# One weight piece split earlier, second norm's statistics as a product with ones, and last layer norm's transposes later, in a hybrid decoder layer

## The chip, the core and the metric

The kernel runs on one core of a Trainium2 chip. The core has five engines with queues of their own, each working through its instructions in order: TensorE (PE; the loading of its weights is shown as PEld), VectorE (DVE), ScalarE (ACT), GpSimd (POOL) and SyncE (SP, which here only starts transfers). PE writes into PSUM; DVE, ACT and POOL work on SBUF, and DVE and ACT also read PSUM. An instruction that needs another engine's result waits for a semaphore, and everything behind it on its engine waits too. The metric is the time of one execution in microseconds (us), the median of several runs.

## What is computed

One decoder layer on 512 tokens of width 2048, in float32. All activations are held transposed: 128 channels on the partitions, 512 tokens along a row.

```python
def reference(x, ...):
    h = rms_norm(x, mix_norm_g[l])
    p = h @ w_in[l]                               # 2048 x 5136
    a_val, a_gate, q, k, v, z, b_raw, a_raw = jnp.split(p, splits, axis=-1)
    out_a = conformer_conv_group(...)             # GLU, conv of 31 taps, layer norm per 128 channels, silu, product
    out_b = gated_deltanet_group(...)             # gated delta rule, chunks
    x = x + jnp.concatenate([out_a, out_b], axis=-1) @ w_out[l]
    h = rms_norm(x, ffn_norm_g[l])                # the second norm
    gate, up = jnp.split(h @ w_up[l], 2, axis=-1) # 2048 x 11264
    gate = causal_depthwise_conv(gate, ffn_conv_w[l]) + ffn_conv_b[l]
    x = x + (jax.nn.silu(gate) * up) @ w_down[l]
    return rms_norm(x, final_norm_g)

def rms_norm(x, g):
    return x * lax.rsqrt(jnp.mean(x * x, axis=-1, keepdims=True) + EPS) * g
```

## The kernel before

Every large product is done in three passes. A weight and an activation are each split into a rounded high half and the remainder: ACT casts the high half (`whi`, `uhi`), DVE subtracts it from the float32 value to get the low half (`wlo`, `ulo`). `mm3` then issues high x high, high x low and low x high, in this order: the first two of three matmuls need only the high half of the weight, the third needs the low one. A **weight piece** is 512 columns of one weight tile, thus four blocks of 128 x 128 and twelve matmuls. `split_piece()` issues the cast and the subtraction of the next piece; the pieces wait in `pieces` until a product takes them. There are four buffers for `hi` and four for `lo`.

The stages in order of time: the input projection with the delta rule and the convolutions beside it; `w_out` for the half that comes from the delta rule (`acc<-obh`), while the last convolution and its layer norm still run; the pointwise product `pw` (`acc<-yh`, 8 tiles); `w_out` for the convolution's half (`acc<-ah`), in the loop `for i, m in enumerate(PAIRS)`, which adds the result to the token tile `xv`; the up projection; the down projection.

The last tile of that loop gives the last token tile. Its consumers are the token operands of the up projection, made by `operand_a` and `operand_b`: ACT scales (`h`), casts (`xb`, `xt`), DVE forms differences (`d`) and low halves. The up projection (`up_out` and the loop `for f in range(NF)`, 44 rounds) computes two rows of two tiles with seven products in place of eight, which is why DVE also adds and subtracts raw weights (`wraw<-uraw,wraw` and the like). In round 0 the products come in the order 11 (into `bx`), 12 (`bv`), 22 (`bz`), s1 and s3 (both halves of `by`), s2 (`bx`), s4 (`bz`), each of 24 matmuls of 256 columns from two pieces; round 1 begins 11 (`bx`), 22 (`bz`), 12 (`bv`), s1 (`by`). Pieces 1 to 4 of round 0 come from `split_piece`, the later ones from `up_products`.

After the seventh product `up_out` multiplies the gate by `rstd2`, the 512 values 1/sqrt(mean square + eps) repeated on all 128 partitions: `fg<-g,rstd_bc` on DVE, once per round. `rstd2` comes from `rms_stats`: four products of the summed squares `sqsum` with a column of ones put the tokens on partitions (128 x 4), DVE scales (`ms`), POOL raises to the power -0.5 (`rstd<-ms,mhalf`), four products with the identity (`statb`) spread the result over the partitions, and ACT copies it to SBUF.

The order of instructions on each engine is fixed when the program is recorded. `Flow` keeps a model clock of each engine; tasks are generators in a heap, `fl.spawn(task, delay)` starts one at a model time, `yield N(tile)` lets it sleep until the model says that the tile is ready, and `fl.tick()` after each `mm3` lets due tasks issue. The model decides only the order; on the chip the semaphores decide the times. `fl.drain(op_ev)` lets the model run until the token operands are issued.

Of the kernel before, what the change touches and what calls it, by code (L numbers as in the profile page):

```python
# [18 lines left out]
ALU = mybir.AluOpType  # L19
AX = mybir.AxisListType  # L20

P = 128
T = 512
NB = 4
D = 2048
KT = D // P
CH = 1024
NC = CH // P
# [7 lines left out]
EPS = 1e-6  # L36
# [9 lines left out]
D_LEFT, D_RIGHT = 40, 4  # L46
SPLIT_TILES = 1
BA_LAG = 3
WARM = 12
ENGINES = {getattr(mybir.EngineType, n) for n in ("PE", "DVE", "Activation", "Pool", "SP")}  # L50

# [240 lines left out]
def N(*aps):  # L292
    return aps, False


def S(*aps):
    return aps, True
# [9 lines left out]
def tile_trunk(ctx: ExitStack, tc: tile.TileContext, xT, w_k, w_ba, w_m, pw, w_out, w_up, w_down, par_d, cst_d, out):  # L307
    nc = tc.nc
    fl = Flow(nc)
    V, ACT, POOL, SP = fl.vector, fl.scalar, fl.gpsimd, fl.sync  # L310
# [19 lines left out]
    def nm(s):  # L330
        uid[0] += 1
        return f"{s}_{uid[0]}"
# [22 lines left out]
    def misc(name="misc"):  # L355
        return fl.tile(misc_ps, [P, T], F32, "misc", 4, nm(name))
# [6 lines left out]
    def alloc(tag, name, shape):  # L363
        fl.live[tag] += 1
        if tag == "misc":
            t = misc(name)
        elif tag == "acc":
            t = fl.tile(acc_ps, [P, T], F32, "acc", 4, nm(name))
        elif tag == "DE":
            t = DE(name, shape)  # L370
        elif tag == "s3":
            t = B(tag, name, shape=(P, 256))
        else:
            t = B(tag, name)
        owner[t.tensor.name] = tag
        return t
# [6 lines left out]
    def turn(tag, n):  # L383
        q = queues.setdefault(tag, deque())
        me = object()
        q.append(me)
        while q[0] is not me or room(tag) < n:
            yield 0.2
        q.popleft()

    def G(tag, name, shape=None):
        yield from turn(tag, 1)
        return alloc(tag, name, shape)
# [5 lines left out]
    def free(*tiles):  # L399
        for t in tiles:  # L400
            fl.live[owner.pop(t.tensor.name)] -= 1
            fl.freed.add(t.tensor.name)
# [6 lines left out]
    def pc(n, i=0, w=1):  # L409
        return par[:, OFF[n] - KT + i : OFF[n] - KT + i + w]  # L410

    def cc(n, w):
        return cst[:, COFF[n] : COFF[n] + w]
# [4 lines left out]
    ones = cc("ones", P)  # L418
    m32 = cc("m32", 64)
    sel = cst[0:32, COFF["sel"] : COFF["sel"] + 16]  # L420
    mhalf = cpool.tile([P, 32], F32, name="mhalf")
# [5 lines left out]
    wps = misc("warm")  # L427
    for _ in range(WARM):
        fl.matmul(wps, lhsT=wz[:, 0:P], rhs=wz)
# [22 lines left out]
    def load_next():  # L452
        i = len(raws)
        if i < (len(plan) if up_done else up_at + 3):
            src, n, step = plan[i]
            raw = fl.tile(wpool, [P, 1024], F32, "raw", 3, nm("wraw"))
            for o in range(0, n, n if i else step):
                e = o + (n if i else step)
                SP.dma_start(raw[:, o:e], src[:, o:e])
            raws.append(raw)  # L460

    def split_piece():
        i, o = nsplit
        if i >= len(plan):
            return
        if i == up_at + 2:
            have = len(pieces)
            for _ in up:
                if len(pieces) > have:
                    return  # L470
                yield
            nsplit[:] = [i + 1, 0]
            i, o = nsplit
        n, step = plan[i][1:]
        w = min(step, n - o)
        src = raws[i][:, o : o + w]
        if i >= len(plan) - 3 * SPLIT_TILES:
            hi, lo = DT("whi"), DT("wlo")
        else:
            hi = fl.tile(wpool, [P, 512], F32R, "hi", 4, nm("whi"))  # L480
            lo = fl.tile(wpool, [P, 512], F32R, "lo", 4, nm("wlo"))
        ACT.copy(out=hi[:, :w], in_=src)
        yield
        V.tensor_tensor(out=lo[:, :w], in0=src, in1=hi[:, :w].bitcast(F32), op=ALU.subtract)
        pieces.append((hi, lo))
        if o + w < n:
            nsplit[1] = o + w
        else:
            nsplit[:] = [i + 1, 0]
            load_next()  # L490
# [97 lines left out]
    def rms_rows(parts, blocks, lag=0.0):  # L588
        yield N(*parts)
        ps = yield from G("misc", "stat")  # L590
        for b in blocks:
            for i, t in enumerate(parts):
                fl.matmul(
                    ps[:, b : b + 1], lhsT=t[:, blk(b)], rhs=ones[:, 0:1], start=i == 0, stop=i == len(parts) - 1)
        n, b0 = len(blocks), blocks[0]
        ms = sm("ms", NB, pool=cpool)
        V.tensor_scalar(out=ms[:, 0:n], in0=ps[:, b0 : b0 + n], scalar1=1.0 / D, scalar2=EPS, op0=ALU.mult, op1=ALU.add)
        free(ps)
        r = rsqrt_pow(ms[:, 0:n], n, "rstd", cpool)
        yield N(r)  # L600
        yield lag
        ps2 = yield from G("misc", "statb")
        for i in range(n):
            fl.matmul(ps2[:, blk(i)], lhsT=r[:, i : i + 1].to_broadcast([P, P]), rhs=ident)
        return r, ps2

    def rms_stats(total, bcast, lag=0.0):
        r, ps2 = yield from rms_rows([total], range(NB), lag)
        ACT.copy(out=bcast, in_=ps2)
        free(ps2)  # L610
        return r

    def rstd_tile(name):
        return fl.tile(cpool, [P, T], F32, "rstdb", 1, name)
# [14 lines left out]
    total = None  # L629
# [37 lines left out]
    for k in range(KT):  # L667
# [9 lines left out]
        if total is None:  # L677
            total = B("cf", "sqsum")
            ACT.activation(out=total, in_=xs, func=AF.Square)
        else:  # L680
            add_square(xs, total, xtmp)
        if k == BA_LAG:
            split_ba()
        if k >= BA_LAG:
            for j in range(0 if k == BA_LAG else k, k + 1):
                ba_product(j)
# [423 lines left out]
    ln_ev = [Event() for _ in range(NC)]  # L1110
# [18 lines left out]
    def conv31(c, u):  # L1129
        a = yield from G("ca", "cacc")  # L1130
        yield S(u)
        ACT.activation(
            out=a, in_=u, func=AF.Identity, scale=pc("dw_w", c * TAPS + TAPS - 1), bias=pc("dw_b", c))
        yield S(a)
        for s in range(1, TAPS):
            V.scalar_tensor_tensor(
                out=a[:, s:], in0=u[:, : T - s], scalar=pc("dw_w", c * TAPS + TAPS - 1 - s), in1=a[:, s:],
                op0=ALU.mult, op1=ALU.add)
            yield 1
        free(u)  # L1140
        fl.spawn(layer_norm(c, a), 0.0, ln_ev[c])

    def layer_norm(c, a):
        tp = yield from transpose4(a)
        free(a)
        bn = sm("bn", NB * 6, 1, pool=bpool)
        mv = sm("mv", NB * 2, pool=bpool)
        for b in range(NB):
            V.bn_stats(out=bn[:, b * 6 : (b + 1) * 6], in_=tp[:, blk(b)])
        for b in range(NB):  # L1150
            V.bn_aggr(out=mv[:, b * 2 : (b + 1) * 2], in_=bn[:, b * 6 : (b + 1) * 6])
        mv2 = mv.rearrange("p (b c) -> p b c", c=2)
        va = sm("va", NB, pool=bpool)
        V.tensor_scalar_add(va.unsqueeze(2), mv2[:, :, 1:2], EPS)
        rl = rsqrt_pow(va, NB, "rl", bpool)
        yield S(rl)
        nmr = sm("nmr", NB, pool=bpool)
        V.scalar_tensor_tensor(
            out=nmr.unsqueeze(2), in0=mv2[:, :, 0:1], scalar=-1.0, in1=rl.unsqueeze(2), op0=ALU.mult, op1=ALU.mult)
        n = yield from G("cf", "lnn")  # L1160
        yield S(nmr)
        for b in range(NB):
            ACT.activation(
                out=n[:, blk(b)], in_=tp[:, blk(b)], func=AF.Identity, scale=rl[:, b : b + 1], bias=nmr[:, b : b + 1])
        free(tp)
        tp2 = yield from transpose4(n)
        free(n)
        y = yield from G("y", "y")
        yield S(tp2)
        ACT.activation(out=y, in_=tp2, func=AF.Silu, scale=pc("ln_g", c), bias=pc("ln_b", c))  # L1170
        SP.dma_start(scr_y[c], y)
        free(tp2, y)
# [79 lines left out]
    for m in PAIRS:  # L1252
        t = fl.tile(opool, [P, T], F32, "xo", 4, nm("xo"))
        SP.dma_start(t, xT[m])
        ps = mtile(obhl)
# [5 lines left out]
    for m in range(NC):  # L1261
        ps = mtile(yhl)
# [3 lines left out]
            out=lo, in0=ps, scalar=pc("pw_b", m), in1=hi.bitcast(F32), op0=ALU.add, op1=ALU.subtract)  # L1266
# [14 lines left out]
    def DT(name):  # L1281
        for pool, n in dpools:
            if fl.live[id(pool)] < n:
                fl.live[id(pool)] += 1
                t = fl.tile(pool, [P, T], F32R, "d", n, nm(name))
                owner[t.tensor.name] = id(pool)
                return t
# [60 lines left out]
    total = [None]  # L1348
# [6 lines left out]
    for i, m in enumerate(PAIRS):  # L1355
        load_xv()
        ps = mtile(ahl)
# [4 lines left out]
        op_ev.append(fl.spawn((operand_b if i % 2 else operand_a)(i // 2, t)))  # L1362
        op_ev.append(fl.spawn(square(t), 1.5))
    rstd2 = rstd_tile("rstd2_bc")
    fl.drain(op_ev)
    fl.spawn(rms_stats(total[0], rstd2, 3.0), 6.0)
    tctx.close()
    actx.close()
    upool = uctx.enter_context(tc.tile_pool(name="up", bufs=1, side="right", reuse_waits="tile"))
# [178 lines left out]
    for f in range(NF):  # L1548
# [7 lines left out]
        for n, w in enumerate(products_of(f)):  # L1556
            b, c, x = products[w]
# [105 lines left out]
    total = None  # L1663
    for m in range(KT - SPLIT_TILES):
        down(1, m)
        total = add_square(x2[m], total, L)
# [110 lines left out]
```

## Time and profile before

| | |
|---|---|
| runs | 2162.17, 2164.89, 2166.77 us, median 2164.89 |
| profiled execution | 2164.05 us, of it 2162.2 us from the first to the last instruction |
| mean granted TensorE clock | 0.996 of full speed |
| busy in the span | PE 2142.8 us (99%), DVE 1626.1 (75%), ACT 956.6 (44%), POOL 60.6 (3%) |
| chain that ended last | PE 95%, DVE 2%, DMA 1% |

The profiled execution is one run, 0.8 us under the median. PE is busy nearly all the time, so what shortens or lengthens the kernel is what PE waits for, and what PE itself does. Matmul rows are pipelined: the distance from one start to the next, and not the row's duration, is what a matmul costs PE. All instructions are recorded in one helper, so their line is always L99; the tile names tell them apart.

### The profile page before, as it was taken

What the parts mean: (1) busy time and instruction counts of PE and PEld (TensorE: products, weight loads), DVE (VectorE), ACT (ScalarE), POOL (GpSimd) and SP (SyncE); (2) the same over time, 40 slices, a digit from 0 to 9 for tenths busy, and PEclk for the clock granted to TensorE, in tenths of its full rate; (3) what the DMA queues carried; (4) which work ended last, traced back from release to release, by engine and by line L of the source; (5) the groups of instructions that cost most, each with busy time, mean ns of one, the idle gap of its engine ahead of it and who ended that gap; (6) DMA issues with size and microseconds to landing.
All of it is one profiled execution on the core that took longest, in us unless ns stands there. A gap on an engine that the chain in (4) does not pass through costs nothing.

```text
span 2162.2 us, 34258 instructions
## 1 busy us (share of the span) xinstructions
PE 2142.8 (99%) x13340; PEld 1929.5 (89%) x13340; DVE 1626.1 (75%) x2692; ACT 956.6 (44%) x1672; POOL 60.6 (3%) x59
## 2 busy tenths in 40 slices
PE   9999999999999999999999999999999999999997
PEld 7888888888788899999999999999999888888886
DVE  6899778887834789999999999999998633344344
ACT  5643544443334655454454555455445422233232
POOL 0310011000000000000000000000000000000000
PEclk9999999999999999999999999999999999999998
DMA  5252333333553533433333333333343733343333
GB/s 199 95 159 98 118 109 107 111 105 120 196 193 132 193 133 110 131 116 112 125 117 114 123 122 108 122 120 112 121 132 123 255 112 120 107 146 90 99 99 112
DMA packets 117618, 276.63 MB, mean 128 GB/s; under 512 B 23376, under 2 KB 36304, under 8 KB 117456
## 3 DMA queue, kind: packets, MB, share of 16 engines
q1 hardware_dynamic: 117312, 274.45, 39.5%
q8 instruction: 104, 1.70, 0.3%
q14 instruction: 58, 0.48, 0.1%
q10 hardware_dynamic: 144, 0.01, 0.0%
HBM read 240.33 MB, written 34.08 MB: 127 GB/s over the span
## 4 chain that ended last, share of the span: by engine, by line
PE 95%; DVE 2%; DMA 1%; issue 1%; ACT 0%; SPq 0%; POOLq 0%; POOL 0%; DVEq 0%; ACTq 0%
PE acc L99 49%; PE by L99 12%; PE bz L99 12%; PE bx L99 12%; PE bv L99 6%; PE tr L99 1%; DVE cacc L99 1%; PE e L99 1%; DMA wraw<-in_w_down_dram 0%; DVE wlo L99 0%; DMA yr<-scr_y 0%; PE pv L99 0%; PE ba L99 0%; PE po L99 0%; PE y L99 0%
## 5 line engine op out<-in xcount | busy, mean ns | idle before, releaser
L99 DVE TENSOR_TENSOR wlo<-wraw,whi 128x512 fp32r<-128x512 f32 (+1 forms) x616 | 414.5, 676 | 318.6 <-ACT whi L99 318.2
L99 ACT CAST whi<-wraw 128x512 fp32r<-128x512 f32 (+1 forms) x616 | 370.9, 607 | 574.3 <-PE acc L99 422.3
L99 PE MATMUL acc<-dh,whi 128*128 128x512 f32 (+1 forms) x726 | 278.0, 383 | 0.4 <-ACT whi L99 0.4
L99 PE MATMUL acc<-dh,wlo 128*128 128x512 f32 (+1 forms) x726 | 277.9, 383 | 0.5 <-DVE wlo L99 0.5
L99 PE MATMUL acc<-dl,whi 128*128 128x512 f32 (+1 forms) x726 | 277.9, 383 | 0.3 <-DVE dl L99 0.3
L99 PE MATMUL acc<-xgh,whi 128*128 128x512 f32 x640 | 260.7, 407 | 0.1
L99 PE MATMUL acc<-xgh,wlo 128*128 128x512 f32 x640 | 250.3, 391 | 0.0
L99 PE MATMUL acc<-xgl,whi 128*128 128x512 f32 x640 | 249.8, 390 | 0.3 <-DVE xgl L99 0.3
L99 DVE SCALAR_TENSOR_TENSOR cacc<-u,par,cacc 128x495 f32<-128x495 f32 (+22 forms) x240 | 173.5, 742 | 1.7 <-ACT cacc L99 0.3
L99 PEld LDWEIGHTS acc<-dh,whi 128*128 128x128 f32 x726 | 136.4, 188 | 27.5 <-ACT whi L99 0.8
L99 PEld LDWEIGHTS acc<-dh,wlo 128*128 128x128 f32 x726 | 136.4, 188 | 27.4 <-DVE wlo L99 0.9
L99 PEld LDWEIGHTS acc<-dl,whi 128*128 128x128 f32 x726 | 136.4, 188 | 27.2 <-DVE dl L99 0.6
L99 ACT CAST uhi<-wraw 128x512 fp32r<-128x512 f32 x176 | 109.4, 622 | 109.4 <-PE by L99 68.2
L99 ACT CAST whi<-uraw 128x512 fp32r<-128x512 f32 x130 | 80.8, 622 | 149.2 <-DVE uraw L99 80.2
L99 DVE TENSOR_TENSOR ulo<-wraw,uhi 128x512 fp32r<-128x512 f32 x176 | 120.8, 687 | 30.6 <-ACT uhi L99 30.6
L99 PEld LDWEIGHTS acc<-xgh,wlo 128*128 128x128 f32 x640 | 120.2, 188 | 26.2
L99 PEld LDWEIGHTS acc<-xgl,whi 128*128 128x128 f32 x640 | 120.6, 189 | 23.1 <-DVE xgl L99 1.0
L99 PEld LDWEIGHTS acc<-xgh,whi 128*128 128x128 f32 x640 | 120.5, 188 | 23.2 <-ACT xgh L99 0.8
L99 PE MATMUL by<-xt,uhi 128*128 128x256 f32 x704 | 130.5, 283 | 0.0
L99 PE MATMUL by<-xt,whi 128*128 128x256 f32 x704 | 130.5, 283 | 0.0
L99 PEld LDWEIGHTS by<-xt,whi 128*128 128x128 f32 x704 | 109.8, 192 | 0.0
L99 PEld LDWEIGHTS by<-xt,uhi 128*128 128x128 f32 x704 | 109.8, 192 | 0.0
(277 smaller groups left out, 4732.1 us busy)
## 6 DMA issues: line engine op xcount, KB each, us to landing
wraw<-in_w_up_dram SPq DMA_DIRECT2D x89, 512.0 KB, 3.9
uraw<-in_w_up_dram SPq DMA_DIRECT2D x87, 512.0 KB, 4.4
wraw<-in_w_m_dram SPq DMA_DIRECT2D x74, 512.0 KB, 3.5
wraw<-in_w_down_dram SPq DMA_DIRECT2D x60, 512.0 KB, 3.5
wraw<-in_w_out_dram SPq DMA_DIRECT2D x32, 512.0 KB, 3.8
wraw<-in_w_down_dram SPq DMA_DIRECT2D x30, 384.0 KB, 3.4
scr_a<-fa SPq DMA_DIRECT2D x44, 256.0 KB, 2.1
dl<-scr_a SPq DMA_DIRECT2D x44, 256.0 KB, 4.9
```

What stands on the lines that cost most here:

```text
L99: return f(**kw) if not args else f(out, *args, **{k: v for k, v in kw.items() if k != "out"})
```

## The change

Three edits. The transposes that begin the layer norm of the last convolution tile are spawned 2.5 us of model time later. One more weight piece, the fourth of round 0, is issued before the model drains the last token operands, thus ahead of them on ACT and DVE. The second norm's statistics no longer go through a 128 x 4 column: one product of an all-ones 128 x 128 matrix with `sqsum` puts the sums on every partition at once, DVE scales all 128 x 512 of them into `rstd2`, and POOL raises all 128 x 512 to the power -0.5 in place. The first and the last norm keep their form.

```diff
+LAST_LAG = 2.5
 ...
-        fl.spawn(layer_norm(c, a), 0.0, ln_ev[c])
+        fl.spawn(layer_norm(c, a), LAST_LAG if c == NC - 1 else 0.0, ln_ev[c])
 ...
     rstd2 = rstd_tile("rstd2_bc")
+    for _ in split_piece():
+        pass
     fl.drain(op_ev)
-    fl.spawn(rms_stats(total[0], rstd2, 3.0), 6.0)
+
+    def second_stats():
+
+        yield N(total[0])
+        ps = yield from G("misc", "stat")
+        fl.matmul(ps, lhsT=ones, rhs=total[0])
+        V.tensor_scalar(out=rstd2, in0=ps, scalar1=1.0 / D, scalar2=EPS, op0=ALU.mult, op1=ALU.add)
+        free(ps)
+        yield S(rstd2)
+        POOL.tensor_tensor(out=rstd2, in0=rstd2, in1=mhalf[:, 0:1].to_broadcast([P, T]), op=ALU.pow)
+
+    fl.spawn(second_stats(), 6.0)
```

PE, where `w_out` for the delta rule's half runs (`acc<-obh`, `acc<-obl`) and the last convolution's output `cacc` is transposed into `tr`. Before:

```order
L99 MATMUL acc_5678<-obh_5273,wlo_5638 128x512
L99 MATMUL tr_5701<-cst,cacc_5356 128x128 x4
L99 MATMUL acc_5678<-obh_5286,whi_5637 128x512
L99 MATMUL acc_5678<-obl_5287,whi_5637 128x512
L99 MATMUL acc_5678<-obh_5286,wlo_5638 128x512
L99 MATMUL acc_5678<-obh_5296,whi_5637 128x512
L99 MATMUL acc_5678<-obl_5297,whi_5637 128x512
L99 MATMUL acc_5678<-obh_5296,wlo_5638 128x512
L99 MATMUL acc_5678<-obh_5300,whi_5637 128x512
L99 MATMUL acc_5678<-obl_5301,whi_5637 128x512
L99 MATMUL acc_5678<-obh_5300,wlo_5638 128x512
L99 MATMUL acc_5737<-obh_5231,whi_5658 128x512
```

The same place in the change:

```order
L100 MATMUL acc_5678<-obh_5273,wlo_5638 128x512
L100 MATMUL acc_5678<-obh_5286,whi_5637 128x512
L100 MATMUL acc_5678<-obl_5287,whi_5637 128x512
L100 MATMUL acc_5678<-obh_5286,wlo_5638 128x512
L100 MATMUL acc_5678<-obh_5296,whi_5637 128x512
L100 MATMUL acc_5678<-obl_5297,whi_5637 128x512
L100 MATMUL acc_5678<-obh_5296,wlo_5638 128x512
L100 MATMUL acc_5678<-obh_5300,whi_5637 128x512
L100 MATMUL acc_5678<-obl_5301,whi_5637 128x512
L100 MATMUL acc_5678<-obh_5300,wlo_5638 128x512
L100 MATMUL tr_5714<-cst,cacc_5356 128x128 x4
L100 MATMUL acc_5737<-obh_5231,whi_5658 128x512
```

The transposes stand nine matmuls later. What hangs on them moves too: on DVE the statistics of this layer norm stand behind one more `wlo`, on ACT its scaling behind one more cast, and on SP the store `scr_y` and the load `yr` each stand behind one more weight load.

DVE, at the end of the loop over `PAIRS`, where the last token tile `xv_7104` is finished and its operands are made; the two `wlo` at the end are the pieces 4 and 5 of the up projection. Before:

```order
L99 TENSOR_TENSOR xv_7104<-xv_7104,acc_7155 128x512
L99 TENSOR_TENSOR sqsum_6485<-sqsum_6485,sq_7201 128x512
L99 TENSOR_TENSOR d_7204<-h_7159 128x512
L99 TENSOR_TENSOR d_7204<-h_7159,d_7204 128x256 x2
L99 TENSOR_TENSOR xb_6415<-h_7159,xb_6415 128x256
L99 TENSOR_TENSOR xt_6399<-d_7204,xt_6399 128x4x256
L99 TENSOR_TENSOR xb_6423<-h_7159,xb_6423 128x256
L99 TENSOR_TENSOR wlo_7227<-wraw_7073,whi_7226 128x512
L99 TENSOR_TENSOR wlo_7238<-wraw_7118,whi_7237 128x512
```

In the change:

```order
L100 TENSOR_TENSOR xv_7104<-xv_7104,acc_7155 128x512
L100 TENSOR_TENSOR wlo_7201<-wraw_7073,whi_7200 128x512
L100 TENSOR_TENSOR sqsum_6485<-sqsum_6485,sq_7205 128x512
L100 TENSOR_TENSOR d_7208<-h_7159 128x512
L100 TENSOR_TENSOR d_7208<-h_7159,d_7208 128x256 x2
L100 TENSOR_TENSOR xb_6415<-h_7159,xb_6415 128x256
L100 TENSOR_TENSOR xt_6399<-d_7208,xt_6399 128x4x256
L100 TENSOR_TENSOR xb_6423<-h_7159,xb_6423 128x256
L100 TENSOR_TENSOR wlo_7235<-wraw_7118,whi_7234 128x512
```

Piece 4 now stands behind the addition into the last token tile, ahead of its operands; its cast on ACT stands ahead of the scaling `h` of that tile in the same way. Piece 5 is unmoved.

POOL, its last instructions (`rl` is the layer norm's power, the two `rstd` of 128 x 2 belong to the last norm). Before:

```order
L99 TENSOR_TENSOR rl_5124<-va_5122,mhalf 128x4
L99 TENSOR_TENSOR rl_5718<-va_5716,mhalf 128x4
L99 TENSOR_TENSOR rstd_7328<-ms_7326,mhalf 128x4
L99 TENSOR_TENSOR rstd_22160<-ms_22158,mhalf 128x2
L99 TENSOR_TENSOR rstd_22247<-ms_22245,mhalf 128x2
```

In the change:

```order
L100 TENSOR_TENSOR rl_5124<-va_5122,mhalf 128x4
L100 TENSOR_TENSOR rl_5731<-va_5729,mhalf 128x4
L100 TENSOR_TENSOR rstd_bc<-rstd_bc,mhalf 128x512
L100 TENSOR_TENSOR rstd_22149<-ms_22147,mhalf 128x2
L100 TENSOR_TENSOR rstd_22236<-ms_22234,mhalf 128x2
```

The third one has 512 columns in place of 4. On PE four products with a 128 x 1 result (`stat`, each two instructions in float32) become one with a 128 x 512 result at the same place, in product 22 of round 0, and the four `statb` in the middle of product s2 are gone, as is ACT's copy of 128 x 512 behind them. DVE's `ms` of 128 x 4 becomes one of 128 x 512 at the same place.

## Rows read from the trace of the kernel before

**Rows 1.** Who PE waited for over the whole span: total, times, longest.

```profile
PE bv L99 <- ACT whi L99: 1.9, 1, 1.9
...
PE tr L99 <- DVE cacc L99: 1.7, 1, 1.7
```

**Rows 2.** Timeline at the last convolution: start, us, engine, operation [idle before <- releaser].

```profile
590.37 0.39 PE L99 MATMUL acc<-obh,wlo 128*128 128x512 f32 x1
...
591.66 0.72 DVE L99 SCALAR_TENSOR_TENSOR cacc<-u,par,cacc 128x482 f32<-128x482 f32 x1
...
592.44 0.65 PE L99 MATMUL tr<-cst,cacc 128*128 128x128 f32 x4 [1.68 <-DVE cacc L99]
```

**Rows 3.** The tile yh: min/median/max ns of one, first and last start.

```profile
L99 PE MATMUL acc<-yh,whi x64: 389/389/389, 639.0 to 681.8; 128*128 128x512 f32 x64
...
L99 DVE TENSOR_TENSOR yl<-yr,yh x8: 680/692/693, 551.9 to 611.5; 128x512 fp32r<-128x512 f32 x8
```

**Rows 4.** Timeline, start of the up projection's round 0.

```profile
770.48 0.73 ACT L99 ACTIVATE h<-xv,par 128x512 f32<-128x512 f32 x1 [2.64 <-DVE xv L99]
...
773.75 0.28 PE L99 MATMUL bv<-xb,wlo 128*128 128x256 f32 x1
...
775.26 1.14 ACT L99 CAST whi<-wraw 128x512 fp32r<-128x512 f32 x2
...
775.93 0.50 PE L99 MATMUL bv<-xb,whi 128*128 128x256 f32 x2 [1.90 <-ACT whi L99]
...
777.30 0.39 PE L99 MATMUL bv<-xb,wlo 128*128 128x256 f32 x1 [0.87 <-DVE wlo L99]
...
779.30 1.70 PE L99 MATMUL stat<-cst,sqsum 128*128 128x1 f32 x8
...
780.86 0.77 PE L99 MATMUL bz<-xt,whi 128*128 128x256 f32 x2
...
785.80 0.68 DVE L99 TENSOR_TENSOR ulo<-uraw,uhi 128x512 fp32r<-128x512 f32 x1
```

**Rows 5.** Windows: length, busy us (instructions) of five engines, PEclk, DMA share, GB/s.

```profile
591.00:592.00 1.00, 0.00 (x0) 0.00 (x0) 1.00 (x3) 0.00 (x0) 0.00 (x0) 1.00 0.00 0
...
779.00:779.50 0.50, 0.50 (x5) 0.50 (x3) 0.50 (x1) 0.00 (x0) 0.00 (x0) 0.50 0.00 0
...
785.50:786.00 0.50, 0.50 (x6) 0.50 (x6) 0.50 (x2) 0.01 (x1) 0.00 (x0) 1.00 0.93 352
...
800.00:1600.00 800.00, 800.00 (x6669) 800.00 (x6668) 734.02 (x1073) 400.72 (x677) 0.00 (x0) 1.00 0.37 119
```

**Rows 6.** Timelines of PE and DVE, product s2 of round 0 until s1 of round 1.

```profile
791.18 0.40 PE L99 MATMUL bx<-xt,whi 128*128 128x256 f32 x2
...
792.62 1.05 PE L99 MATMUL statb<-cst,rstd 128*128 128x128 f32 x8
793.42 0.48 PE L99 MATMUL bx<-xt,uhi 128*128 128x256 f32 x2
...
799.75 0.69 DVE L99 TENSOR_TENSOR fg<-g,rstd_bc 128x512 f32<-128x512 f32 x1
800.36 0.69 DVE L99 TENSOR_TENSOR wlo<-wraw,whi 128x512 fp32r<-128x512 f32 x1
...
806.46 0.40 PE L99 MATMUL by<-xt,whi 128*128 128x256 f32 x2
```

**Rows 7.** Powers and one multiplication on POOL, by tile and on the timeline.

```profile
L99 POOL TENSOR_TENSOR rl<-va,mhalf x8: 1007/1010/1297, 211.6 to 594.7; 128x4 f32<-128x4 f32 x8
...
70.65 1.04 POOL L99 TENSOR_TENSOR slgh<-cst,graw_h 128x512 fp32r<-128x512 f32 x1
...
786.97 1.39 POOL L99 TENSOR_TENSOR rstd<-ms,mhalf 128x4 f32<-128x4 f32 x1 [190.99 <-DVE ms L99]
...
2150.84 0.70 POOL L99 TENSOR_TENSOR rstd<-ms,mhalf 128x2 f32<-128x2 f32 x1 [8.30 <-DVE ms L99]
...
2151.59 1.22 PE L99 MATMUL statb<-cst,rstd 128*128 128x128 f32 x4 [1.10 <-POOL rstd L99]
```

## Prediction

> **What bounds the kernel now.** I read the page's totals first: PE is busy 99% of the span, so the kernel gains only where PE waits, idles its clock or does less. Then the table of PE's waits. Two entries belong to this change: PE waited 1.9 us for a weight's high half before a product into `bv`, and 1.7 us for the last convolution before its transposes [rows 1]. Then the timelines around both places, and the windows, for the granted clock. The reader is to see three things there. At 590 us PE is held by DVE's last step of the convolution, with the clock at full speed throughout [rows 2, 5]. At 774 to 777 us PE is held first by ACT's cast and then by DVE's subtraction of the fourth weight piece [rows 4]; after it the granted clock is 0.50 (1.2 GHz) in the window at 779 us and back at 1.00 (2.4 GHz) in the one at 785.5 us [rows 5]. From 800 to 1600 us PE has no idle time at all and DVE is busy 734 of 800 us [rows 5]: DVE has little room, and what blocks DVE there blocks PE once the weight pieces in hand are used up. Last I read POOL, because the change gives it its only large new job.
>
> All times below are on the clock of the trace of before, so they leave out what edit 3 has saved by then. The sum is made against the profiled execution, 2164.05 us, which lies 0.8 us under the median of the runs.
>
> **Transposes of the last layer norm.** A matmul of 512 columns costs PE (681.8 - 639.0) / 189 = 0.2265 us from start to start: 64 blocks of three, thus 189 steps [rows 3]. The one at 590.37 is followed at 590.60 by the transposes, which start at 592.44 [rows 2]: 1.84 us lost. Nine matmuls moved ahead are 2.04 us of work, so PE reaches the transposes at 592.64, after the convolution's end at 591.66 + 0.72 = 592.38 [rows 2]. The wait is covered with 0.26 us to spare: **-1.84**. Behind it the layer norm's statistics, its scaling, the store and the load each move behind one more piece or load, some 3 us at twelve matmuls a piece. That costs nothing: its last result `yl` was made at 611.5 us and its tile is first read at 639.0 at the earliest [rows 3]; 24 us would have to go before PE felt it.
>
> **The fourth weight piece.** Before, its cast is the first of two at 775.26, behind all operands of the last token tile [rows 4]. Now it stands ahead of them, where ACT sat idle 2.64 us for `xv` [rows 4], and DVE's subtraction goes between `xv` and the sum of squares, which waits for ACT's square anyhow: both cost nothing there. Without that cover the subtraction would delay the operands by its 0.6 us. The buffer is free only once the last `w_out` matmul has read it, and `xv` waits for that same matmul. What is late next is piece five, whose cast and subtraction stay behind the operands. PE ends the first half of `bv` at 773.87, does the second at 0.12 us a matmul (twelve from 791.18 to 792.62 [rows 6]) until 775.31, waits until 775.93 for the fifth high half, issues two matmuls and waits until 777.30 for its low half: the two moments at which before it got the fourth [rows 4]. So PE still idles 0.62 + 1.13 us in place of 2.06 + 1.13.
>
> The clock decides how much this is worth. At 590 us PE idled 1.84 us in one stretch and the clock stayed at full [rows 2, 5]; the 3.2 us here were followed by half speed. 1.75 us in two parts is nearer to the first, so I take the clock as staying up. Then count from 777.30 to the start of product s2, 13.88 us before (791.18 [rows 6]): 22 matmuls of `bz` (2.64), the new statistics (0.80, below), 48 of `by` (5.76), and one wait: DVE, now 0.60 us earlier by one subtraction, ends the tenth piece at 785.80 + 0.68 - 0.60 = 785.88 [rows 4], PE wants it at 785.30, 0.6 us late. That is 9.82 us: **-4.06**, with the products of the statistics in it. If the clock falls all the same, only the twelve matmuls remain: -1.44.
>
> **Statistics on PE, ACT and DVE.** The four old column products hold PE from 779.30 to 780.86, 1.56 us at half clock [rows 4]. No float32 product with 512 columns is in the trace; the nearest is `statb`, four of 128 columns, which hold PE from 792.62 to 793.42, 0.80 us [rows 6], taken for the new one and in the count above. `statb` itself goes: **-0.80**. ACT loses a copy that nothing misses; DVE's `ms` grows from 4 columns to 512, by something between nothing and the 0.69 us of DVE's whole rows of that length [rows 6]; I take +0.6, which delays the pieces for s2 by that much and PE by under 0.1 us.
>
> **The power on POOL.** This is the term that decides. POOL raised 128 x 4 in 1.007 us undisturbed, 1.39 us beside a busy DVE, and 128 x 2 in 0.70 us [rows 7]. These are real durations: `statb` waited for the last of them and started at 2151.59, 0.05 us after its end [rows 7]. Two columns more cost 0.307 us, so 0.1535 us a column; for 512 columns 1.007 + 508 x 0.1535 = **79 us**. No power longer than four columns is in the trace. The cheap end is a multiplication of 128 x 512, 1.04 us; the dear end is 1.39 us for every four columns, 178 us [rows 7]. I take 79: it is the slope between two sizes of the same operation, and the multiplication is another one.
>
> It starts at 786.97 [rows 7], since DVE comes there 0.60 us earlier and its `ms` is 0.6 us longer, and ends at 866.0. Its first reader is `fg<-g,rstd_bc` of round 0 on DVE, which would come at 799.75 - 4.86 = 794.89 [rows 6]: DVE waits 71 us. Behind it on DVE stands at once the subtraction (800.36 before) for the piece that PE begins at 806.46 with product s1 of round 1 [rows 6]; behind it on ACT, `fa` and then the next casts. PE works through the pieces that it has and wants that low half at 806.46 - 4.86 + 0.24 = 801.84. It comes at 866.0 + 0.05 + 0.61 + 0.69 + 0.05 = 867.4 (0.05 us for each semaphore, as `statb` shows). PE waits **65.6 us**. Before, DVE was 5.65 us ahead of PE here (done at 801.05, wanted at 806.70 [rows 6]); after the wait it is ahead by nothing, and with 92% to do [rows 5] it regains that partly out of PE's time, partly while PE's clock comes back up: between 0 and 5.65 us, I take **+3**.
>
> **Sum.** 2164.05 - 1.84 - 4.06 - 0.80 + 65.6 + 3 = 2225.95, thus 2226 us.
>
> **Rivals.**
>
> First, the power is cheap on a long row and ends before 794.89 (8 us or less). For it: POOL may work through many columns faster than through two or four, which no row tells, and POOL multiplies 512 columns in 1.04 us [rows 7]. Against it: the two sizes differ by far more than a multiplication of all 512. Then 2164.05 - 6.70 = 2157.4, faster; with the clock still falling 2160.0. The Trainium skill (GPSIMD Engine Reference, section 3.1, Elementwise) gives 2.6 cycles an element for a two-input tensor_tensor on POOL at 1.2 GHz, an estimate of 1.1 us for 512 columns; it says it of an addition, and by that rule the sum would be this rival's. The multiplication's row agrees with it, the powers' rows don't.
>
> Second, between: a long power has cheaper columns, but not that cheap. PE is spared up to 801.84, a power of 13.5 us; from there each microsecond counts, and at about 20 us the kernel is where it was before. At 40 us it would take 2157.35 + 26.5 + 3 = 2187.
>
> Third, dearer: DVE disturbs POOL all along and every four columns take 1.39 us; 178 us give some 2325. Against it: DVE itself stands still from 795 us on, with nothing to disturb.
>
> That edit 1 merely moves its wait (2.6 us less saved) changes no sign and lies in the range.
>
> **Numbers.** The linear power 0.77, the cheap one 0.12, the one between 0.07, the dearer 0.04. The likeliest case alone spans 2212 to 2250: 0.13 to 0.2 us a column, and 0 to 6 us for the lead. The range reaches down to 2168 to take in most of the case between, which holds 0.8 in all. About 0.2% (4.3 us) is what a measurement of this kernel can tell from no change. Faster: the cheap case, 0.12; the same: powers near 20 us, 0.03; slower: 0.85.
>
> **What would show it.** Right: one POOL row of 128 x 512 near 79 us from about 785 us; DVE idle some 71 us before the first `fg`, released by POOL; PE idle some 65 us before a `by` matmul that waits for a `wlo`; no wait before the transposes of `cacc`; a clock of 1.00 from 777 to 790 us. Wrong: a POOL row under 14 us, with which PE has no long wait at all. The steps are separate: the first two may hold while the third fails.

## The result and the profile after

The changed kernel takes 2229.67 us (2228.57 to 2230.87, 6 runs) against 2164.09 us (2162.17 to 2168.03, 6 runs) on the same chip: a ratio of 1.0301, 95% interval 1.029 to 1.0312, 65.6 us slower. The prediction was 2226 us, range 2168 to 2250. The profiled execution took 2230.24 us, 66.19 us more than that of before.

The page first: totals, three of the rows in 40 slices of 55.7 us, and the shares of the chain that ended last.

```profile
PE 2142.6 (96%) x13326; PEld 1928.1 (87%) x13326; DVE 1626.6 (73%) x2692; ACT 954.4 (43%) x1671; POOL 141.2 (6%) x59
...
PE   9999999999999933999999999999999999999997
...
POOL 0310011000000085000000000000000000000000
PEclk9999999999999976999999999999999999999998
...
PE 92%; POOL 4%; DVE 2%; issue 1%; DMA 0%; ACT 0%; SPq 0%; POOLq 0%; DVEq 0%; ACTq 0%
```

One hole in PE's row, at slices 15 and 16, and in the same two slices POOL's only dense activity. POOL has 4% of the chain that ended last. Who PE waited for, and the timelines of POOL, DVE, ACT and PE around the hole:

```profile
PE by L100 <- DVE wlo L100: 68.3, 1, 68.3
...
PE acc L100 <- DVE wlo L100: 1.0, 1, 1.0
PE acc L100 <- ACT whi L100: 0.9, 1, 0.9
PE bz L100 <- DVE wlo L100: 0.9, 1, 0.9
PE bz L100 <- ACT whi L100: 0.5, 1, 0.5
```

```profile
785.62 82.31 POOL L100 TENSOR_TENSOR rstd_bc<-rstd_bc,mhalf 128x512 f32<-128x512 f32 x1 [188.81 <-DVE rstd_bc L100]
...
867.96 0.69 DVE L100 TENSOR_TENSOR fg<-g,rstd_bc 128x512 f32<-128x512 f32 x1 [68.09 <-POOL rstd_bc L100]
868.57 0.69 DVE L100 TENSOR_TENSOR wlo<-wraw,whi 128x512 fp32r<-128x512 f32 x1
...
868.69 0.81 ACT L100 ACTIVATE fa<-fg,par 128x512 f32<-128x512 f32 x1 [69.28 <-DVE fg L100]
...
869.31 0.58 PE L100 MATMUL by<-xt,wlo 128*128 128x256 f32 x1 [68.28 <-DVE wlo L100]
...
874.17 0.39 PE L100 MATMUL by<-xt,whi 128*128 128x256 f32 x2
```

Read from the top, this is a chain of three waits with one cause. POOL's power ends at 867.93; `fg`, which reads it, starts 0.03 us later, and DVE had stood still 68.09 us for it. The subtraction behind `fg` reads nothing of the power, but stands behind it on its engine; PE resumes 0.05 us after it. In the kernel before, the same `fg` and subtraction ran back to back without a wait [rows 6], and POOL's power took 1.39 us [rows 7].

The places of the other two edits: the end of the last convolution on DVE and the transposes behind it on PE, then PE at the start of the up projection.

```profile
592.43 0.72 DVE L100 SCALAR_TENSOR_TENSOR cacc<-u,par,cacc 128x482 f32<-128x482 f32 x1
...
592.80 0.39 PE L100 MATMUL acc<-obh,wlo 128*128 128x512 f32 x1
593.20 0.66 PE L100 MATMUL tr<-cst,cacc 128*128 128x128 f32 x4
...
774.67 0.50 PE L100 MATMUL bz<-xt,whi 128*128 128x256 f32 x2 [0.46 <-ACT whi L100]
776.04 0.39 PE L100 MATMUL bz<-xt,wlo 128*128 128x256 f32 x1 [0.87 <-DVE wlo L100]
776.26 1.02 PE L100 MATMUL stat<-sqsum,cst 128*128 128x512 f32 x2
...
777.35 0.28 PE L100 MATMUL bz<-xt,wlo 128*128 128x256 f32 x1
```

In front of the transposes the page counts no wait, where it counted 1.68 us before [rows 2]. By the starts 0.40 us lie between them and the matmul before, 0.17 more than the 0.23 of a matmul of 512 columns: the convolution's last step ended only at 593.15, thus just too late. And the waits of 1.90 and 0.87 us in front of `bv` [rows 4] became 0.46 and 0.87 in front of `bz`. The granted clock by windows (eighth column):

```profile
779.00:780.00 1.00, 1.00 (x11) 1.00 (x10) 1.00 (x2) 0.07 (x1) 0.00 (x0) 1.00 0.00 0
...
804.00:805.00 1.00, 0.00 (x0) 0.00 (x0) 0.00 (x0) 0.00 (x0) 1.00 (x1) 1.00 0.00 0
805.00:806.00 1.00, 0.00 (x0) 0.00 (x0) 0.00 (x0) 0.00 (x0) 1.00 (x1) 0.94 0.00 0
866.00:867.00 1.00, 0.00 (x0) 0.00 (x0) 0.00 (x0) 0.00 (x0) 1.00 (x1) 0.50 0.00 0
873.00:874.00 1.00, 1.00 (x7) 1.00 (x7) 1.00 (x2) 0.00 (x0) 0.00 (x0) 0.50 0.71 246
874.00:875.00 1.00, 1.00 (x10) 1.00 (x10) 1.00 (x3) 0.58 (x2) 0.00 (x0) 0.92 0.11 45
```

It is 1.00 (2.4 GHz) at 779 us, where it was 0.50 before [rows 5]. It falls to 0.50 (1.2 GHz) while PE waits for the power, and stays there until 874 us, behind the wait: the 22 matmuls from 869.31 to 874.17 take 4.86 us, where 22 at 0.12 us, the rate of [rows 6], are 2.64.

### The profile page after: what moved, and what is told of

Read it like the earlier page. It is cut to its first block, busy times and chain, and to the rows that moved or that the text cites. A ratio compares the mean times of both kernels' runs of the same rounds, so it can differ in the third digit from the quotient of the medians.

```text
span 2228.4 us, 34228 instructions
## 1 busy us (share of the span) xinstructions
PE 2142.6 (96%) x13326; PEld 1928.1 (87%) x13326; DVE 1626.6 (73%) x2692; ACT 954.4 (43%) x1671; POOL 141.2 (6%) x59
## 4 chain that ended last, share of the span: by engine, by line
PE 92%; POOL 4%; DVE 2%; issue 1%; DMA 0%; ACT 0%; SPq 0%; POOLq 0%; DVEq 0%; ACTq 0%
PE acc L100 51%; PE by L100 11%; PE bz L100 11%; PE bx L100 11%; PE bv L100 5%; POOL rstd_bc L100 4%; PE tr L100 1%; PE e L100 1%; DVE wlo L100 0%; PE pv L100 0%; PE ba L100 0%; DVE ulo L100 0%; PE po L100 0%; PE y L100 0%; PE psn L100 0%
## 5 line engine op out<-in xcount | busy, mean ns | idle before, releaser
L100 PE MATMUL by<-xt,wlo 128*128 128x256 f32 x352 | 100.5, 286 | 68.3 <-DVE wlo L100 68.3
L100 PEld LDWEIGHTS by<-xt,wlo 128*128 128x128 f32 x352 | 68.2, 194 | 68.7 <-DVE wlo L100 68.7
```

What stands on the lines that cost most here:

```text
L100: return f(**kw) if not args else f(out, *args, **{k: v for k, v in kw.items() if k != "out"})
```

## Experiments

The theory is the prediction's: all of the loss is the power's length, through DVE's order and PE's wait, and the other parts gain a little. Its rivals: the product with ones or the wide broadcast costs something by itself; the power has a large fixed part; what is gained at the other edits is given back. Each kernel was compared with the kernel before on its own chip.

**Without the statistics edit, and the statistics edit alone.** `no_stats_edit` takes the second edit out of the changed kernel:

```diff
-    def second_stats(): ...
-    fl.spawn(second_stats(), 6.0)
+    fl.spawn(rms_stats(total[0], rstd2, 3.0), 6.0)
```

> Edits 1 and 3 alone, the second norm's statistics as before. Theory A (the whole loss is the power of 128 x 512 on POOL, and the other two edits gain): the two waits are gone, the clock stays up, and only the four products statb stay: 2164.1 - 1.8 - 3.6 = 2158.7 us, ratio 0.9975. Rival B (the other two edits do not gain, or cost): 2164 us or more. If the clock still falls after the shortened wait: about 2161 us.

Measured: 2160.33 us (11 runs) against 2164.41 us, ratio 0.998 (0.9972 to 0.9989). Rival B falls. The time is near the 2161 us named for a clock that still falls, and in the trace it did (below). `stats_edit_alone` takes the other two out:

```diff
-for _ in split_piece():
-    pass
-        fl.spawn(layer_norm(c, a), LAST_LAG if c == NC - 1 else 0.0, ln_ev[c])
+        fl.spawn(layer_norm(c, a), 0.0, ln_ev[c])
```

> Edit 2 alone. Theory A: POOL's power takes 82.3 us as in the whole change and its end sets everything behind it; it starts some 1.9 us later than in the whole change, so 2229.7 + 1.9 = 2231.6 us: the other edits' gains upstream of the power count only as far as they let it start earlier. Rival B (the edits add up, each with its own gain): 2164.1 + 71 = 2235 us.

Measured: 2232.23 us (4 runs) against 2164.41, ratio 1.0314 (1.03 to 1.0328). So the whole loss comes with the statistics; the other two edits gain 4.1 us without it. The rival, that the edits' gains add up (2235 us), falls too: the other two edits are worth only about what they let the power start earlier (785.62 against 788.03 us). POOL's power again takes 82.31 us; PE's wait is a little shorter, since PE comes there later:

```profile
871.72 0.58 PE L99 MATMUL by<-xt,wlo 128*128 128x256 f32 x1 [66.74 <-DVE wlo L99]
```

**The power's length as a dose.** Four kernels keep the whole change, and with it the product with ones, DVE's wide `ms` and the broadcast by 128 partitions. Three raise only the first columns to the power, the fourth multiplies all 512 in its place:

```diff
-        POOL.tensor_tensor(out=rstd2, in0=rstd2, in1=mhalf[:, 0:1].to_broadcast([P, T]), op=ALU.pow)
+        POOL.tensor_tensor(
+            out=rstd2[:, 0:64], in0=rstd2[:, 0:64], in1=mhalf[:, 0:1].to_broadcast([P, 64]), op=ALU.pow)
```

> The whole change, but POOL raises only the first 64 of the 512 columns to the power; the power of the other 448 is left out. Theory A (0.16 us a column): POOL takes 1.0 + 60 x 0.16 = 10.6 us, is done at about 796 us, before DVE's first reader at about 800 us: no wait for it, 2158 us. Rival (the price is one of the instruction, or of its place, and not of its columns): about 2230 us.

> The whole change, but the power on the first 128 of 512 columns only (384 left out). At 0.16 us a column the power takes 21 us from 785.6 to about 806.6 us, DVE waits some 7 us for it in front of the gate's product, and PE some 6 to 7 us at the next weight piece: 2160 + 6.5 = about 2166.5 us, just slower than before. If the power had a fixed part, or cost less for each column on wider tiles, it would come out near 2160 us.

> The whole change, but the power on the first 256 of 512 columns only (256 left out). At 0.16 us a column 41.5 us, to about 827 us: PE waits about 27 us, and with about 2 us of half clock behind it 2189 us. The time should rise by PE's wait alone between 128, 256 and 512 columns, some 20.5 us and then 41 us.

> The whole change with a multiplication in place of the power, same tiles, same 128 x 512, same place; the power is left out. Theory A: POOL takes 1.0 to 1.5 us, DVE does not wait, 2158 us. Rival (POOL beside DVE, the in-place write or the order costs the time, not the power): still above 2200 us.

POOL's row and PE's wait for the `wlo` behind it, of 64 columns, of 128, of 256, and of the multiplication, in this order:

```profile
785.63 10.90 POOL L100 TENSOR_TENSOR rstd_bc<-rstd_bc,mhalf 128x64 f32<-128x64 f32 x1 [188.82 <-DVE rstd_bc L100]
...
804.40 0.39 PE L100 MATMUL by<-xt,wlo 128*128 128x256 f32 x1 [0.66 <-DVE wlo L100]
```

```profile
786.19 21.10 POOL L100 TENSOR_TENSOR rstd_bc<-rstd_bc,mhalf 128x128 f32<-128x128 f32 x1 [188.84 <-DVE rstd_bc L100]
...
808.67 0.58 PE L100 MATMUL by<-xt,wlo 128*128 128x256 f32 x1 [7.25 <-DVE wlo L100]
```

```profile
785.14 41.50 POOL L100 TENSOR_TENSOR rstd_bc<-rstd_bc,mhalf 128x256 f32<-128x256 f32 x1 [189.22 <-DVE rstd_bc L100]
...
828.02 0.58 PE L100 MATMUL by<-xt,wlo 128*128 128x256 f32 x1 [27.67 <-DVE wlo L100]
```

```profile
785.67 1.42 POOL L100 TENSOR_TENSOR rstd_bc<-rstd_bc,mhalf 128x512 f32<-128x512 f32 x1 [188.96 <-DVE rstd_bc L100]
...
801.18 0.39 PE L100 MATMUL by<-xt,wlo 128*128 128x256 f32 x1 [0.28 <-DVE wlo L100]
...
805.09 0.39 PE L100 MATMUL by<-xt,wlo 128*128 128x256 f32 x1 [0.77 <-DVE wlo L100]
```

| POOL's operation | its us | PE's wait, us | time, us | before, us | ratio, 95% interval |
|---|---|---|---|---|---|
| multiplication, 512 columns | 1.42 | 0.28, 0.77 | 2160.78 | 2164.41 | 0.9983 (0.9974 to 0.9992) |
| power, 64 | 10.90 | 0.66 | 2159.88 | 2164.41 | 0.998 (0.997 to 0.9989) |
| power, 128 | 21.10 | 7.25 | 2168.07 | 2163.19 | 1.002 (1.0011 to 1.0029) |
| power, 256 | 41.50 | 27.67 | 2188.93 | 2163.19 | 1.0118 (1.0105 to 1.0132) |
| power, 512 | 82.31 | 68.28 | 2229.67 | 2164.09 | 1.0301 (1.029 to 1.0312) |

The four powers lie on one line: (21.10 - 10.90) / 64, (41.50 - 21.10) / 128 and (82.31 - 41.50) / 256 are all 0.159 us a column, with 0.7 us beside it. From 128 columns on PE's wait is the power less 13.8 to 14.0 us. So the first 14 us of a power are free, and from there PE pays each microsecond. The multiplication keeps the product with ones, the broadcast, the in-place write and the place on POOL, and gains; so none of these is the cause. A large fixed part of the power is ruled out by the line.

The run of 128 columns came out 1.6 us over its expectation. Its windows show what that left out:

```profile
803.00:804.00 1.00, 0.00 (x0) 0.00 (x0) 0.00 (x0) 0.00 (x0) 1.00 (x1) 0.91 0.00 0
807.00:808.00 1.00, 0.00 (x0) 0.00 (x0) 0.67 (x2) 0.00 (x0) 0.29 (x1) 0.50 0.00 0
812.00:813.00 1.00, 1.00 (x7) 1.00 (x6) 1.00 (x2) 0.00 (x0) 0.00 (x0) 0.50 1.01 324
814.00:815.00 1.00, 1.00 (x10) 1.00 (x10) 1.00 (x3) 1.00 (x3) 0.00 (x0) 0.97 0.00 0
```

The wait of 7.25 us is followed by half clock from 808.67 to about 814 us, some 5 us as behind the wait of 68.28 us; behind the 27.67 us it is some 4 us. Counted like the 22 matmuls above, that costs 1.9 to 2.4 us, whatever the wait. The transposes of this execution also waited again:

```profile
593.74 0.66 PE L100 MATMUL tr<-cst,cacc 128*128 128x128 f32 x4 [0.66 <-DVE cacc L100]
```

**The other two edits, one at a time.** `piece_alone` and `lag_alone` put one of them into the kernel before:

```diff
+    for _ in split_piece():
+        pass
     fl.drain(op_ev)
```

> Edit 1 alone: the fourth weight piece of the first round ahead of the last token operands; statistics and last layer norm as in the kernel before. The wait at 775 us shrinks from 2.77 us in two parts to about 1.4 us. If the granted clock still falls behind it, as in the run with edits 1 and 3, only that is saved: 2164.4 - 1.4 to 2.3 = about 2162.5 us. If the clock stays at 1.00, as the prediction has it, about 2160.8 us.

```diff
+LAST_LAG = 2.5
-        fl.spawn(layer_norm(c, a), 0.0, ln_ev[c])
+        fl.spawn(layer_norm(c, a), LAST_LAG if c == NC - 1 else 0.0, ln_ev[c])
```

> Edit 3 alone: only the last layer norm's transposes stand nine matmuls later. Prediction's theory: the wait of 1.68 us at 592.44 us is gone and nothing takes its place: 2164.4 - 1.8 = 2162.6 us. Rival: what is won there is given back at a later wait for weights: 2164.4 us.

Measured, against 2164.38 us (33 runs): 2161.59 us for the piece, ratio 0.9985 (0.9975 to 0.9994), and 2162.17 us for the transposes, ratio 0.9989 (0.998 to 0.9998). Both gain, 2.8 and 2.2 us, and together (above) 4.1. The rival of `lag_alone`, that its gain is given back, falls. In the trace of `piece_alone` the waits are 0.46 and 0.87 us, but the granted clock fell behind them all the same, to 0.50 from 780 to 783 us. So it did in `no_stats_edit`, while it stayed at 1.00 in the changed kernel behind the same two waits.

**What lets the clock fall.** These two traces, in which it fell behind the short waits, have the old column products (the narrow ones of the expectations below) one matmul behind them; the changed kernel, in which it stayed, has the wide product there. `stats_later` is `no_stats_edit` with the old statistics placed later; `before_stats_later` is the kernel before with the same:

```diff
-    fl.spawn(rms_stats(total[0], rstd2, 3.0), 6.0)
+    fl.spawn(rms_stats(total[0], rstd2, 3.0), 9.0)
```

> Edits 1 and 3 with the old statistics, whose four one-column products now stand some ninety matmuls later, not right behind the wait at 775 us. If the narrow products right behind the wait are what lets the granted clock fall: clock 1.00 from 770 to 790 us and about 2158.3 us. If the wait itself does: the clock falls as in the run with edits 1 and 3, about 2160.3 us.

> The kernel before, all three edits undone, but with the second norm's statistics placed later, so that the four one-column products don't stand right behind the wait at 775 us, which keeps its 2.77 us. If the narrow products right behind the wait are what let the granted clock fall, it stays at 1.00 and the time is about 2162 us; if a wait of this length is enough, it falls all the same and the time is 2164.4 us.

In both the column products came to stand 24 matmuls later, not some ninety. One window behind the wait in each, first of `no_stats_edit`, then of `stats_later`, then of `before_stats_later`:

```profile
777.00:778.00 1.00, 1.00 (x5) 1.00 (x6) 0.46 (x1) 0.46 (x1) 0.00 (x0) 0.50 0.00 0
```

```profile
777.00:778.00 1.00, 1.00 (x11) 1.00 (x10) 0.40 (x1) 0.51 (x1) 0.00 (x0) 1.00 0.00 0
```

```profile
779.00:780.00 1.00, 1.00 (x10) 1.00 (x9) 0.44 (x1) 0.47 (x1) 0.00 (x0) 1.00 0.00 0
```

Two more traces belong beside these. First the kernel before, whose first column product starts at 779.30 us [rows 4]; then `stats_edit_alone`, which has the full wait and the wide product:

```profile
778.50:779.00 0.50, 0.50 (x5) 0.50 (x4) 0.50 (x1) 0.00 (x0) 0.00 (x0) 0.53 0.00 0
```

```profile
778.00:779.00 1.00, 1.00 (x6) 1.00 (x7) 0.99 (x2) 0.00 (x0) 0.00 (x0) 0.52 0.00 0
...
780.65 1.42 PE L99 MATMUL stat<-sqsum,cst 128*128 128x512 f32 x2
```

Behind the full wait of 2.77 us the clock fell before any product of the statistics was issued, column or wide; so it did in `lag_alone`. So the products are not what let it fall there. In `before_stats_later` PE issues the same instructions up to that place, and the clock stayed at 1.00: behind the same wait it fell in one execution and not in another.

Behind the two short waits the traces do divide by the products: it fell in both with the column products right behind (`no_stats_edit`, `piece_alone`) and stayed in all seven without them (the changed kernel, `stats_later`, `sqrt`, the multiplication and the three shorter powers).

The times say less: `stats_later` 2160.59 us (ratio 0.9982, 0.9974 to 0.9991), no better than `no_stats_edit`; `before_stats_later` 2163.38 against 2163.19 us, ratio 1.0 (0.9991 to 1.0009), so no gain. A part of the answer is in both traces, first of `stats_later`, then of `before_stats_later`:

```profile
785.86 3.19 POOL L100 TENSOR_TENSOR rstd<-ms,mhalf 128x4 f32<-128x4 f32 x1 [189.88 <-DVE ms L100]
...
789.10 1.16 PE L100 MATMUL statb<-cst,rstd 128*128 128x128 f32 x8 [1.62 <-POOL rstd L100]
```

```profile
791.14 1.16 PE L99 MATMUL statb<-cst,rstd 128*128 128x128 f32 x8 [0.61 <-POOL rstd L99]
```

Now the power of four columns was late (3.19 us in both), and PE waited 1.62 and 0.61 us for it. `before_stats_later` has another answer in the list of its runs: the profiled execution, with 2161.5 us and a mean granted clock of 0.998, is the fastest of 11; eight of the others have 0.996 and two 0.997. So its profile shows an exception.

How much the mean clock differs from execution to execution of one kernel, the 33 runs of the kernel before beside `stats_later` show: nine with a mean clock of 0.997 took 2162.2 us on average, eight with 0.996 2163.6, ten with 0.995 2165.0, six with 0.994 2168.4. Averaged over all runs of a kernel, the mean clock is 0.9975 in `sqrt`, 0.9974 in `stats_later`, 0.9971 in `power_64_columns` and `multiply_512`, 0.9965 in `no_stats_edit` and `piece_alone`, 0.9964 in `before_stats_later`, 0.9962 in `lag_alone`, and between 0.9956 and 0.996 in the kernel before, by the chip. Against the kernel before on the same chip, the kernels with the short waits and without column products behind them gain 0.0011 to 0.0018, those with the short waits alone 0.0005 and 0.0009, that with the later products alone 0.0004, and `lag_alone`, which changes neither, 0.0006. That fits a clock that stays up more often with both, worth 1 to 2 us by estimate (some 0.0005 to 0.001 of 2160 us); but only the traces tell where the clock fell, and the times don't show such a gain (2159.88 to 2160.78 us with both, 2160.33 for `no_stats_edit`). What in the column products matters behind a short wait (their 128 x 1 results, or where they stand) was not taken apart.

**Without POOL.** `sqrt` is the whole change with the power split between two other engines:

```diff
-        POOL.tensor_tensor(out=rstd2, in0=rstd2, in1=mhalf[:, 0:1].to_broadcast([P, T]), op=ALU.pow)
+        ACT.activation(out=rstd2, in_=rstd2, func=AF.Sqrt)
+        yield S(rstd2)
+        V.reciprocal(rstd2, rstd2)
```

> The whole change, but the power on 512 columns is made a square root on ACT and a reciprocal on DVE. ACT takes about 0.6 us and a table load before and after, DVE's reciprocal 0.7 to 5.7 us (from the reciprocal of 32 columns, 354 ns, in the kernel before). DVE waits 2.9 us for a weight load before it comes to the gate's product, so most of that is hidden: theory (all of the loss was the power) about 2160 us; if the product with ones or the wide broadcast also costs, above 2164.4 us.

Measured: 2160.1 us (2158.32 to 2161.5, 11 runs) against 2164.38, ratio 0.998 (0.9972 to 0.9989). On ACT and DVE:

```profile
786.26 1.28 ACT L100 ACT_TABLE_LOAD   x1
787.55 0.63 ACT L100 ACTIVATE rstd_bc<-rstd_bc 128x512 f32<-128x512 f32 x1
```

```profile
788.22 3.35 DVE L100 RECIPROCAL rstd_bc<-rstd_bc 128x512 f32<-128x512 f32 x1 [0.24 <-ACT rstd_bc L100]
```

The same 512 columns cost 0.63 + 3.35 us and two table loads of 1.28 us (the second for the activation that follows) in place of 82.31 us, and lie for the most part where DVE otherwise stands 2.88 us for a cast that in its turn waits for a weight load. PE's longest wait in the up projection is 0.9 us. This computes the whole layer and beats both kernels; it is level with leaving the statistics as they were (2160.33 us).

## Why the prediction was right

**The power** was the deciding term and had the right form: the slope between two and four columns, 0.1535 us, carried to 512 gave 79 us; measured 82.31, at 0.159 us a column. The first rival's rule, that POOL takes a long row cheaply, holds for the multiplication only: 512 columns of it took 1.42 us here, the power of the same row 58 times that. The Trainium skill (GPSIMD Engine Reference, section 3.1, Elementwise) has 2.6 cycles an element, which it says of an addition; at 1.2 GHz that is an estimate of 1.1 us for 512 columns, near the multiplication and far from the power. The third rival's dearer columns did not come either: the 64 columns, raised while DVE was busy 8.0 of 10.9 us, lie on the same line as the last columns of the long power, beside which DVE stood still.

**The chain through DVE** held instruction for instruction. DVE waited 68.09 us (predicted 71), PE 68.28 (65.6). PE wanted the low half at 869.31 - 68.28 = 801.03; the prediction had that moment at 801.84 on the clock of before, thus 1.84 less, 800.0, on its own. It got it at 869.31 where 867.4 - 1.84 = 865.56 was predicted, 3.3 of the 3.75 us by the longer power. DVE's own arrival at `fg` was misjudged: with PE 6.7 us earlier DVE should have come at 793, but was free for it at 799.20 + 0.68 = 799.88, no earlier than before [rows 6]. The traces show why, that of before first:

```profile
792.07 0.62 ACT L99 CAST whi<-wraw 128x512 fp32r<-128x512 f32 x1 [3.01 <-DMA wraw<-in_w_up_dram]
```

```profile
792.22 0.62 ACT L100 CAST whi<-wraw 128x512 fp32r<-128x512 f32 x1 [5.18 <-DMA wraw<-in_w_up_dram]
...
792.88 0.69 DVE L100 TENSOR_TENSOR wlo<-wraw,whi 128x512 fp32r<-128x512 f32 x1 [2.88 <-ACT whi L100]
...
799.20 0.68 DVE L100 TENSOR_TENSOR g<-u,bz 128x512 f32<-128x512 f32 x1
```

The weight load sets the pace there, and it came at 792 us before as well. Behind an 82-us power this cost nothing; in the short powers it does.

**What the free cases gain** was the term most overestimated. The three edits without the power's price were put at 6.70 us. PE reached the low half's matmul 806.70 - 801.03 = 5.67 us earlier in the changed kernel, but `multiply_512`, `power_64_columns` and `sqrt` gain 3.6, 4.5 and 4.3 us. Part is given back right there: in `multiply_512` PE waits 0.28 and 0.77 us for low halves in the two products of round 1 into `by`, where before it waited for none. With that the break-even lies lower than the 20 us of the second rival: 10.90 us of power gain 4.5 us, 21.10 us lose 4.9. A power of 14 us is still free, and a wait carries the 2 us of half clock with it, which gives about 16 us as an estimate.

**The new product** held PE 0.85 us (776.26 to 777.35, less two matmuls of 0.12), where 0.80 were taken from `statb`.

**The transposes** gained 2.2 us by the run alone, where 1.84 were predicted. The 0.26 us to spare were less sure than they look: the convolution's end lay anywhere from 591.9 to 593.7 us in the traces, and the transposes still lost 0.17 us in the changed kernel and waited 0.66 us in the run of 128 columns. **The fourth piece** made the two short waits predicted (0.46 and 0.87 us on the page, 0.62 and 1.13 counted from start to start). The step on the clock is the one whose reason failed: "1.75 us in two parts is nearer to the first, so I take the clock as staying up". It stayed up in the profile of after, but with the old products behind it, the same wait let it fall in two traces, and behind the full wait it fell in three traces and stayed in one. So the wait's length alone does not decide, and that the step came true is in part luck.

**The lead after the wait** was put at +3: measured 66.19 + 5.67 - 68.28 = 3.58 us, of which 4.86 - 2.64 = 2.22 is the half clock until 874.17. The rest comes later, partly in the waits of 1.0 and 0.9 us for weight halves in the down projection's products into `acc`, which were 0.5 and 0.4 us before.

Between the profiled executions the sum fell 66.19 - 61.9 = 4.3 us short: PE resumed 3.75 us later than predicted, 3.3 of it by the power, and the lead was 0.6 more. That PE came to the wait 1.0 us later than predicted cost nothing, since it waited there anyhow. For the same reason the time is no test of the terms -4.06 and -0.80: what they take from PE's way to the wait, they add to the wait. Only their own rows and the runs without the long power test them.

## What to carry to other kernels

Before an elementwise operation is widened to save a broadcast, look for two sizes of the same operation on the same engine in the trace and take the slope; another operation's price says nothing, 1.42 against 82.31 us here. An engine that is hardly used can still stop the kernel: find the first reader of its result, see what stands behind that reader in its queue, and ask for how long the next engine has work in hand (14 us here). A gain of a few microseconds that rests on the granted clock wants the clock of many runs, not of one profile.

## What the runs showed of the hardware

POOL's power costs 0.159 us for each column of 128 partitions from 64 to 512 columns; 128 x 4 took 1.01 to 1.39 us in the kernel before [rows 7], and 3.19 us where it was placed a little later. Whether DVE, busy beside it for most of those 3.19 us, held POOL up was not tried; the power of 64 columns beside a busy DVE shows no such delay. DVE's own reciprocal of 128 x 512 took 3.35 us, about five times a subtraction of that size (0.69).

A stretch at half clock behind a wait was some 5 us long behind 7 and behind 68 us of waiting, some 4 us behind 28. Behind the same wait of 2.77 us, and the same instructions of PE, it came in one execution and not in another. The kernel before spread over some 6 us with its mean clock, from 2162.2 us at 0.997 to 2168.4 at 0.994. One stretch like that of its profile, from 778.5 to 785.5 us [rows 5], costs some 3.5 us by its length, an estimate, and so can't make all of that; where the rest lies no trace shows.
